# A contrast kernel on one core: the first slot of its ring holds two half tiles instead of one tile

## The chip, the cores and the metric

The kernel runs on one core of a Trainium2 chip. The other cores do nothing. The time is in device microseconds (us), lower is better; each version is run several times, and the median is taken. One further execution is recorded by the hardware profiler: its trace holds every instruction and every DMA packet with start and length.

The engines that matter here are VectorE (DVE in the profile), ScalarE (ACT), TensorE (PE), GpSimd (POOL) and SyncE (SP). SP issues the loads, ACT issues the stores, and 16 DMA engines move the bytes of both queues.

## What is computed

```python
def setup_inputs():
    batch, c, h, w = 16, 3, 512, 512
    return {
        "x": np.random.rand(batch, c, h, w).astype(np.float32),
        "factor": np.float32(1.5),
    }

def reference(x, factor):
    mean = np.mean(x, axis=(2, 3), keepdims=True)
    return np.clip(mean + factor * (x - mean), 0, 1).astype(np.float32)
```

There are 48 images (16 x 3) of 262,144 pixels in float32, 50.33 MB in and as much out. Every pixel becomes factor * x + (1 - factor) * mean of its image, held between 0 and 1. An image's mean must be known before any of its pixels can be written.

## The kernel before

The input lies in DRAM as one run of numbers. A tile is four images, 4.19 MB, spread over 128 partitions with 8192 numbers (32 KB) in each, so that one image covers 32 partitions. There are 12 tiles. A ring in SBUF, `ring` (L66), has six slots of one tile; tile t lives in slot t mod 6 and is changed in place.

The body is under `tc.manual_schedule()` (L103): the instructions of every engine stand in the order in which the program writes them, and the framework adds the semaphore waits.

- **Loads** (L68 to L76) go out on SP's queue. Tile 0 comes in two DMAs, columns 0 to 2047 (1 MB) and 2048 to 8191 (3 MB), L104 and L105; tile 1 in one; tiles 2 and 3 in one DMA of 8 MB, and tiles 4 and 5 in another (L107, L108). After computing tile t, SP is given the load of tile t + 6 (L112), which waits until the stores of tile t have read their slot. SP's queue runs in order, so a load that waits holds up the loads behind it.
- **Compute** (L78 to L98) of a tile: VectorE sums columns 0 to 4351 of each partition (L81, `SUM` = 4352) while ScalarE sums the other 3840 by an activation with an accumulator (L84; what it writes goes to `junk` and is not used). Two matrix products with the constant `blockw` (L86, L87) add the partial sums over the 32 partitions of each image, scale them by (1 - factor) / pixels, and leave the shift of each partition in PSUM (`bias`). VectorE then does x * factor + shift over the whole tile (L91) and the clamp (L94).
- **Stores** (L101) go out on ACT's queue, one DMA of 4 MB a tile. Tile 0 is the exception: `FIRST` = (2048, 6144) makes it do L91, L94 and the store for the first 2048 columns and then for the other 6144, so that it has two stores of 1 MB and 3 MB. ACT's queue holds sum, store, sum, store; the store of a tile waits for L94 of that tile.
- **Constants**: GpSimd fills `blockw` (L61, L63) at the start: zero, and four 32x32 blocks on the diagonal.

In DRAM a partition's 32 KB follow on those of the partition before. A store or load of a whole tile is therefore one unbroken stretch of 4 MB; the two parts of tile 0 take 8 KB and 24 KB out of every 32 KB.

Of the kernel before, what the change touches and what calls it, by code (L numbers as in the profile page):

```python
# [1 line left out]

# [4 lines left out]


P = 128  # L10
ROW = 8192
BUFS = 6
SHORT = 2048
FIRST = (SHORT, ROW - SHORT)
SUM = 4352


@with_exitstack
def kernel(
    ctx: ExitStack,  # L20
    tc: tile.TileContext,
    x: bass.AP,
    factor: float,
    out: bass.AP,
):

    nc = tc.nc
    f32 = mybir.dt.float32  # L30
    Alu = mybir.AluOpType
    Act = mybir.ActivationFunctionType

    B, C, H, W = x.shape
    n_img, n_pix = B * C, H * W
    ppi = n_pix // ROW
    per_tile = P // ppi
    n_tiles = n_img // per_tile
    assert ppi * ROW == n_pix and per_tile * n_tiles == n_img

    factor = float(factor)
    wconst = (1.0 - factor) / float(n_pix)

    x_f = x.rearrange("b c h w -> (b c h w)")
    out_f = out.rearrange("b c h w -> (b c h w)")

    def dram(ap, t, c0=0, c1=ROW):
        return bass.AP(tensor=ap.tensor, offset=t * P * ROW + c0, ap=[[ROW, P], [1, c1 - c0]])

    consts = ctx.enter_context(tc.tile_pool(name="consts", bufs=1))  # L50
    xpool = ctx.enter_context(tc.tile_pool(name="xpool", bufs=1))
    small = ctx.enter_context(tc.tile_pool(name="small", bufs=1))
    psum = ctx.enter_context(tc.tile_pool(name="psum", bufs=1, space=bass.MemoryType.PSUM))


    sums = small.tile([P, 2 * n_tiles], f32, name="sums")
    junk = small.tile([P, ROW - SUM], f32, name="junk")
    bias = psum.tile([P, n_tiles], f32, name="bias")

    blockw = consts.tile([P, P], f32, name="blockw")  # L60
    nc.gpsimd.memset(blockw, 0.0)  # L61
    for a in range(0, P, ppi):
        nc.gpsimd.memset(blockw[a : a + ppi, a : a + ppi], wconst)  # L63


    ring = xpool.tile([P, BUFS, ROW], f32, name="ring")  # L66

    def load(t, c0=0, c1=ROW, n=1):  # L68

        b = t % BUFS  # L70
        src = bass.AP(
            tensor=x_f.tensor,
            offset=t * P * ROW + c0,
            ap=[[ROW, P], [P * ROW, n], [1, c1 - c0]],
        )
        nc.sync.dma_start(out=ring[:, b : b + n, c0:c1], in_=src)  # L76

    def compute(t):  # L78
        xt = ring[:, t % BUFS, :]
        own = sums[:, 2 * t : 2 * t + 2]  # L80
        nc.vector.tensor_reduce(  # L81
            out=own[:, 0:1], in_=xt[:, 0:SUM], axis=mybir.AxisListType.X, op=Alu.add
        )
        nc.scalar.activation(out=junk, in_=xt[:, SUM:ROW], func=Act.Copy, accum_out=own[:, 1:2])  # L84
        shift = bias[:, t : t + 1]
        nc.tensor.matmul(shift, blockw, own[:, 1:2], start=True, stop=False)  # L86
        nc.tensor.matmul(shift, blockw, own[:, 0:1], start=False, stop=True)  # L87
        c = 0
        for n in FIRST if t == 0 else [ROW]:
            part = xt[:, c : c + n]  # L90
            nc.vector.tensor_scalar(  # L91
                out=part, in0=part, scalar1=factor, scalar2=shift, op0=Alu.mult, op1=Alu.add
            )
            nc.vector.tensor_scalar(  # L94
                out=part, in0=part, scalar1=0.0, scalar2=1.0, op0=Alu.max, op1=Alu.min
            )
            store(t, c, c + n)
            c += n  # L98

    def store(t, c0, c1):  # L100
        nc.scalar.dma_start(out=dram(out_f, t, c0, c1), in_=ring[:, t % BUFS, c0:c1])  # L101

    with tc.manual_schedule():  # L103
        load(0, c1=SHORT)  # L104
        load(0, c0=SHORT)  # L105
        load(1)
        load(2, n=2)  # L107
        load(4, n=2)  # L108
        for t in range(n_tiles):
            compute(t)  # L110
            if t + BUFS < n_tiles:
                load(t + BUFS)  # L112


# [1 line left out]
_INS = ['x', 'factor']  # L116
_OUTS = [((16, 3, 512, 512), 'float32')]

_NUMBERS = {'factor': 1.5}


# [26 lines left out]
```

## Time and profile before

| what | value |
|---|---|
| time, three runs | 239.05, 239.31, 240.11 us (median 239.31) |
| span of the profiled execution | 237.3 us |
| bytes read, written | 50.33 MB, 50.33 MB |
| mean rate over the span | 424 GB/s |
| VectorE busy | 163.1 us (69%) |
| ScalarE busy | 43.2 us (18%) |
| TensorE busy | 14.1 us (6%) |
| loads on SP, stores on ACT | 11 DMAs, 13 DMAs |

The span runs from the first to the last event of the program in the profiler's record; the time of a run is taken around it and is longer. The profiled execution is one of its own, and its time beyond the span is not recorded: 2.0 us lie between its span and the median of the three runs.

The profile's page divides the span into 40 equal slices and prints for each the busy share of each engine in tenths (9 is 90% or more) and the rate in GB/s. It lists the DMA queues with their packets; one packet is one row of a transfer, or one of 4 bytes that signals a semaphore. Then comes the chain of waits that ended last, and the groups of instructions by line, with the mean time of one. Of DMA issues it gives the time from issue to landing:

```profile
out_dram<-ring ACTq DMA_DIRECT2D x11, 4096.0 KB, 35.8
ring<-in_x_dram SPq DMA_DIRECT2D x7, 4096.0 KB, 49.7
ring<-in_x_dram SPq DMA_DIRECT2D x2, 8192.0 KB, 66.7
ring<-in_x_dram SPq DMA_DIRECT2D x1, 3072.0 KB, 11.7
out_dram<-ring ACTq DMA_DIRECT2D x1, 3072.0 KB, 28.2
ring<-in_x_dram SPq DMA_DIRECT2D x1, 1024.0 KB, 4.8
out_dram<-ring ACTq DMA_DIRECT2D x1, 1024.0 KB, 17.5
```

The columns are what is moved, the queue, how many DMAs, the size of each, and the median time to landing in us. A transfer that stands behind others in its queue shows their time too.

### The profile page before, as it was taken

The numbers are of one execution on the slowest core, as the hardware profiler recorded it, in microseconds if no ns is written. First come the engines' busy times: TensorE is split into PE (matmuls) and PEld (weight loads), VectorE is DVE, ScalarE is ACT, GpSimd is POOL, SyncE is SP. The second block draws the span as 40 slices with busy tenths as digits, with TensorE's granted clock in tenths as the row PEclk, the third lists the DMA queues.
The fourth block names the chain that finished last, engine by engine and source line by source line (L and its number), as shares of the span: only waits on it lengthen the run. The fifth ranks groups of instructions, "written<-read, shape, count | busy, mean of one in ns | idle before, by whom it ended". The sixth has DMA issues, their size and how long they took to land.

```text
span 237.3 us, 285 instructions
## 1 busy us (share of the span) xinstructions
PE 14.1 (6%) x48; PEld 12.0 (5%) x48; DVE 163.1 (69%) x38; ACT 43.2 (18%) x25; POOL 0.9 (0%) x9
## 2 busy tenths in 40 slices
PE   0010010001010001010010100100100100010000
PEld 0010010001010001010010100100100100010000
DVE  0079989048989328999989898891892795687000
ACT  2050230041050023050320504101400500500000
POOL 1000000000000000000000000000000000000000
DMA  7999999999999999999999999999999999999996
GB/s 297 410 442 442 421 442 359 456 439 441 442 436 414 403 431 442 442 442 442 436 442 436 414 409 425 442 442 442 442 436 442 436 420 403 425 442 442 442 442 265
DMA packets 3712, 100.66 MB, mean 424 GB/s; under 512 B 384, under 2 KB 384, under 8 KB 384
## 3 DMA queue, kind: packets, MB, share of 16 engines
q1 hardware_dynamic: 1840, 50.33, 49.7%
q10 hardware_dynamic: 1872, 50.33, 49.2%
HBM read 50.33 MB, written 50.33 MB: 424 GB/s over the span
## 4 chain that ended last, share of the span: by engine, by line
DMA 57%; DVE 29%; another core or an unknown queue 3%; PE 1%; SPq 1%; issue 0%; DVEq 0%
DMA ring<-in_x_dram 41%; DMA out_dram<-ring 16%; DVE sums L81 10%; DVE ring L91 9%; DVE ring L94 9%; PE bias L87 1%; SPq L76 1%; DVEq L91 0%
## 5 line engine op out<-in xcount | busy, mean ns | idle before, releaser
L81 DVE TENSOR_REDUCE sums<-ring 128x1 f32<-128x4352 f32 x12 | 56.2, 4683 | 45.7 <-DMA ring<-in_x_dram 45.7
L84 ACT ACTIVATE junk<-ring 128x3840 f32<-128x3840 f32 x12 | 40.8, 3403 | 163.3 <-DMA ring<-in_x_dram 107.5
L91 DVE TENSOR_SCALAR ring<-ring,bias 128x8192 f32<-128x8192 f32 (+2 forms) x13 | 54.1, 4163 | 8.9 <-PE bias L87 7.4
L94 DVE TENSOR_SCALAR ring<-ring 128x8192 f32<-128x8192 f32 (+2 forms) x13 | 53.3, 4099 | 0.4
L86 PE MATMUL bias<-sums,blockw 128*128 128x1 f32 x24 | 7.0, 361 | 190.8 <-ACT junk L84 190.8
L86 PEld LDWEIGHTS bias<-sums,blockw 128*128 128x128 f32 x24 | 6.0, 312 | 191.7 <-ACT junk L84 175.2
L87 PE MATMUL bias<-sums,blockw 128*128 128x1 f32 x24 | 7.0, 363 | 4.3 <-DVE sums L81 3.9
L87 PEld LDWEIGHTS bias<-sums,blockw 128*128 128x128 f32 x24 | 6.0, 311 | 5.3 <-DVE sums L81 5.0
L84 ACT ACTIVATION_READ_ACCUMULATOR junk<-ring 128x1 f32 x12 | 2.2, 186 | 0.0
L84 ACT ACT_TABLE_LOAD x1 | 1.3, 1283 | 0.7 <-PEq L129 0.7
L63 POOL MEMSET blockw<- 32x32 f32 x4 | 0.5, 117 | 0.2
L61 POOL MEMSET blockw<- 128x128 f32 x1 | 0.2, 204 | 0.3 <-POOLq L129 0.3
L129 POOL MEMSET const-bfloat16-1.0<- 128x1 bf16 x1 | 0.1, 111 | 0.0
L129 POOL MEMSET const-uint8-127<- 128x1 uint8 x1 | 0.1, 111 | 0.0
L129 POOL MEMSET const-float32-1.0<- 128x1 f32 x1 | 0.1, 108 | 0.0
L129 POOL MEMSET const-float32-0.0<- 128x1 f32 x1 | 0.1, 103 | 0.2 <-issue 0.2
## 6 DMA issues: line engine op xcount, KB each, us to landing
out_dram<-ring ACTq DMA_DIRECT2D x11, 4096.0 KB, 35.8
ring<-in_x_dram SPq DMA_DIRECT2D x7, 4096.0 KB, 49.7
ring<-in_x_dram SPq DMA_DIRECT2D x2, 8192.0 KB, 66.7
ring<-in_x_dram SPq DMA_DIRECT2D x1, 3072.0 KB, 11.7
out_dram<-ring ACTq DMA_DIRECT2D x1, 3072.0 KB, 28.2
ring<-in_x_dram SPq DMA_DIRECT2D x1, 1024.0 KB, 4.8
out_dram<-ring ACTq DMA_DIRECT2D x1, 1024.0 KB, 17.5
```

Of the source, the lines that this page charges most:

```text
L61: nc.gpsimd.memset(blockw, 0.0)
L63: nc.gpsimd.memset(blockw[a : a + ppi, a : a + ppi], wconst)
L76: nc.sync.dma_start(out=ring[:, b : b + n, c0:c1], in_=src)
L81: nc.vector.tensor_reduce(out=own[:, 0:1], in_=xt[:, 0:SUM], axis=mybir.AxisListType.X, op=Alu.add)
L84: nc.scalar.activation(out=junk, in_=xt[:, SUM:ROW], func=Act.Copy, accum_out=own[:, 1:2])
L86: nc.tensor.matmul(shift, blockw, own[:, 1:2], start=True, stop=False)
L87: nc.tensor.matmul(shift, blockw, own[:, 0:1], start=False, stop=True)
L91: nc.vector.tensor_scalar(out=part, in0=part, scalar1=factor, scalar2=shift, op0=Alu.mult, op1=Alu.add)
L94: nc.vector.tensor_scalar(out=part, in0=part, scalar1=0.0, scalar2=1.0, op0=Alu.max, op1=Alu.min)
L129: nc = _bacc.Bacc("TRN2", target_bir_lowering=False, num_devices=1)
```

## The change

The work is divided by images instead of by fixed rows. `TILES` gives the images of each tile: two tiles of two images, then eleven of four, 13 tiles in all. `IMG` = 2048 is what one image takes in every partition when it is spread over all 128, so a tile of n images has rows of n * 2048 numbers: 16 KB for the first two, 32 KB for the others. The ring becomes one run of columns; the first two tiles share slot 0, and tile 7 is the next to use that slot.

- Tiles 0 and 1 are each loaded by one DMA of 2 MB and stored by one of 2 MB. In a two-image tile an image covers 64 partitions, so there is a second constant matrix, with two 64x64 blocks.
- The loads up front are tile 0, tile 1, tile 2, tiles 3 and 4 together, tiles 5 and 6 together. Nothing is loaded after computing tile 0; after tile 1 comes the load of tile 7, which waits for the stores of both half tiles, and so on to tile 12.
- VectorE's share of the summing is 35/64 of a row: 4480 columns of 8192, and 2240 of 4096. ScalarE has the other 3712 or 1856.
- L91 and L94 (now L97 and L100) run over the whole tile in every case; the split of tile 0 is gone.

```diff
-ROW = 8192
-BUFS = 6
-SHORT = 2048
-FIRST = (SHORT, ROW - SHORT)
-SUM = 4352
+IMG = 2048
+SLOTS = 6
+
+TILES = (2, 2) + (4,) * 11
+
+SHARE = 35
...
+    first = [sum(TILES[:t]) for t in range(n_tiles)]
+    columns = SLOTS * 4 * IMG
...
+    block = {}
+    for n in sorted(set(TILES)):
+        rows = P // n
+        block[n] = m = consts.tile([P, P], f32, name=f"block{n}")
+        nc.gpsimd.memset(m, 0.0 if n > 1 else wconst)
+        for a in range(0, P, rows) if n > 1 else ():
+            nc.gpsimd.memset(m[a : a + rows, a : a + rows], wconst)
...
+    def cols(t):
+        a = first[t] * IMG % columns
+        return ring[:, a : a + TILES[t] * IMG]
...
+    def dram(ap, t, n=1):
+        row = TILES[t] * IMG
+        return bass.AP(
+            tensor=ap.tensor, offset=first[t] * n_pix, ap=[[row, P], [P * row, n], [1, row]]
+        )
...
+    def load(t, n=1):
+        a = first[t] * IMG % columns
+        row = TILES[t] * IMG
+        dst = ring[:, a : a + n * row].rearrange("p (n r) -> p n r", r=row)
+        nc.sync.dma_start(out=dst, in_=dram(x_f, t, n))
...
     def compute(t):
-        xt = ring[:, t % BUFS, :]
+        xt = cols(t)
+        row = TILES[t] * IMG
+        vec = row * SHARE // 64
...
-        c = 0
-        for n in FIRST if t == 0 else [ROW]:
-            part = xt[:, c : c + n]
-            nc.vector.tensor_scalar(
-                out=part, in0=part, scalar1=factor, scalar2=shift, op0=Alu.mult, op1=Alu.add
-            )
-            nc.vector.tensor_scalar(
-                out=part, in0=part, scalar1=0.0, scalar2=1.0, op0=Alu.max, op1=Alu.min
-            )
-            store(t, c, c + n)
-            c += n
...
+        nc.scalar.dma_start(
+            out=dram(out_f, t), in_=xt.rearrange("p (n r) -> p n r", n=1)
+        )
...
     with tc.manual_schedule():
-        load(0, c1=SHORT)
-        load(0, c0=SHORT)
+        load(0)
         load(1)
-        load(2, n=2)
-        load(4, n=2)
+        load(2)
+        load(3, n=2)
+        load(5, n=2)
         for t in range(n_tiles):
             compute(t)
-            if t + BUFS < n_tiles:
-                load(t + BUFS)
+            if t >= 1 and t + SLOTS < n_tiles:
+                load(t + SLOTS)
```

More of the change, by code (lines that the diff above doesn't have):

```diff
@@ L34 @@
     B, C, H, W = x.shape
[L35 to L39, printed above, removed]
+    n_pix = H * W
+    assert n_pix == P * IMG and sum(TILES) == B * C
     factor = float(factor)
@@ L45 @@
     out_f = out.rearrange("b c h w -> (b c h w)")
-    def dram(ap, t, c0=0, c1=ROW):
-        return bass.AP(tensor=ap.tensor, offset=t * P * ROW + c0, ap=[[ROW, P], [1, c1 - c0]])
+    n_tiles = len(TILES)
+    first = [sum(TILES[:t]) for t in range(n_tiles)]
+    columns = SLOTS * 4 * IMG
     consts = ctx.enter_context(tc.tile_pool(name="consts", bufs=1))
@@ L56 @@
     sums = small.tile([P, 2 * n_tiles], f32, name="sums")
-    junk = small.tile([P, ROW - SUM], f32, name="junk")
+    junk = small.tile([P, 4 * IMG * (64 - SHARE) // 64], f32, name="junk")
     bias = psum.tile([P, n_tiles], f32, name="bias")
[L60 to L74, printed above, removed]
-        )
-        nc.sync.dma_start(out=ring[:, b : b + n, c0:c1], in_=src)
+    block = {}
@@ new lines @@
+    for n in sorted(set(TILES)):
[4 more added lines that the diff above has]
+            nc.gpsimd.memset(m[a : a + rows, a : a + rows], wconst)
+    ring = xpool.tile([P, columns], f32, name="ring")
+    def cols(t):
[5 more added lines that the diff above has]
+            tensor=ap.tensor, offset=first[t] * n_pix, ap=[[row, P], [P * row, n], [1, row]]
+        )
@@ L78, in compute @@
+    def load(t, n=1):
[3 more added lines that the diff above has]
+        nc.sync.dma_start(out=dst, in_=dram(x_f, t, n))
     def compute(t):
-        xt = ring[:, t % BUFS, :]
+        xt = cols(t)
+        row = TILES[t] * IMG
+        vec = row * SHARE // 64
         own = sums[:, 2 * t : 2 * t + 2]
         nc.vector.tensor_reduce(
-            out=own[:, 0:1], in_=xt[:, 0:SUM], axis=mybir.AxisListType.X, op=Alu.add
+            out=own[:, 0:1], in_=xt[:, 0:vec], axis=mybir.AxisListType.X, op=Alu.add
@@ L83, in compute @@
         )
-        nc.scalar.activation(out=junk, in_=xt[:, SUM:ROW], func=Act.Copy, accum_out=own[:, 1:2])
+        nc.scalar.activation(
+            out=junk[:, 0 : row - vec], in_=xt[:, vec:row], func=Act.Copy, accum_out=own[:, 1:2]
+        )
         shift = bias[:, t : t + 1]
-        nc.tensor.matmul(shift, blockw, own[:, 1:2], start=True, stop=False)
-        nc.tensor.matmul(shift, blockw, own[:, 0:1], start=False, stop=True)
-        c = 0
-        for n in FIRST if t == 0 else [ROW]:
-            part = xt[:, c : c + n]
-            nc.vector.tensor_scalar(
-                out=part, in0=part, scalar1=factor, scalar2=shift, op0=Alu.mult, op1=Alu.add
-            )
-            nc.vector.tensor_scalar(
-                out=part, in0=part, scalar1=0.0, scalar2=1.0, op0=Alu.max, op1=Alu.min
-            )
-            store(t, c, c + n)
-            c += n
@@ L100, in store @@
-    def store(t, c0, c1):
-        nc.scalar.dma_start(out=dram(out_f, t, c0, c1), in_=ring[:, t % BUFS, c0:c1])
+        nc.tensor.matmul(shift, block[TILES[t]], own[:, 1:2], start=True, stop=False)
+        nc.tensor.matmul(shift, block[TILES[t]], own[:, 0:1], start=False, stop=True)
+        nc.vector.tensor_scalar(
+            out=xt, in0=xt, scalar1=factor, scalar2=shift, op0=Alu.mult, op1=Alu.add
+        )
+        nc.vector.tensor_scalar(
+            out=xt, in0=xt, scalar1=0.0, scalar2=1.0, op0=Alu.max, op1=Alu.min
+        )
@@ L103 @@
+        nc.scalar.dma_start(
+            out=dram(out_f, t), in_=xt.rearrange("p (n r) -> p n r", n=1)
+        )
     with tc.manual_schedule():
-        load(0, c1=SHORT)
-        load(0, c0=SHORT)
+        load(0)
         load(1)
-        load(2, n=2)
-        load(4, n=2)
+        load(2)
+        load(3, n=2)
+        load(5, n=2)
         for t in range(n_tiles):
             compute(t)
-            if t + BUFS < n_tiles:
-                load(t + BUFS)
+            if t >= 1 and t + SLOTS < n_tiles:
+                load(t + SLOTS)
```

## The prediction, made before the change was run

> **What bounds the kernel now.** I read the time slices first, then the DMA part, then busy time in three long stretches, and only then the chain of waits.
>
> ```profile
> DVE  0079989048989328999989898891892795687000
> ...
> DMA  7999999999999999999999999999999999999996
> ...
> DMA packets 3712, 100.66 MB, mean 424 GB/s; under 512 B 384, under 2 KB 384, under 8 KB 384
> ...
> DMA 57%; DVE 29%; another core or an unknown queue 3%; PE 1%; SPq 1%; issue 0%; DVEq 0%
> ```
>
> The DMA engines are busy in every slice but the two at the ends; VectorE has holes of whole slices. So the chain's "DVE 29%" misleads: a chain must pass through some work, but while VectorE computes, the 16 engines move other tiles. What counts is bytes over rate plus the moments when the engines are not full.
>
> ```profile
> 0.00:60.00 60.00, 3.49 (x12) 3.01 (x12) 35.98 (x10) 11.77 (x7) 0.88 (x9) 1.00 0.97 411
> 60.00:203.70 143.70, 9.39 (x32) 8.02 (x32) 113.49 (x26) 27.97 (x16) 0.00 (x0) 1.00 1.01 434
> 203.70:237.30 33.60, 1.18 (x4) 1.01 (x4) 13.60 (x3) 3.50 (x2) 0.00 (x0) 1.00 0.94 406
> ```
>
> The columns are stretch, length, busy time of the engines, clock, DMA share and GB/s. With both streams running the rate is 434. At that rate 100.66 MB take 100.66/0.434 = 231.9 us; the span is 237.3, so 5.4 us are lost in all: 60 x (1 - 411/434) = 3.2 in the first 60 us, 33.6 x (1 - 406/434) = 2.2 in the last stretch, none between. The packet records of the same trace (start, length, bytes, queue) place them. At the start: first packet at 1.74 us, then 0.7 until all engines run at their usual packet time. Near 24 to 28 us and 37.7 to 39.3 us, 0.8 together: load packets of 32 KB, otherwise 1.213 us, take up to 1.508 and 1.792. At the end: 0.4 because the engines do not finish together and 1.25 after the last packet (236.05). These are 4.9 of the 5.4; the rest is rounding and edges of the windows.
>
> ```profile
> 12.96 4.69 DVE L81 TENSOR_REDUCE sums<-ring 128x1 f32<-128x4352 f32 x1 [12.96 <-DMA ring<-in_x_dram]
> 20.91 7.06 ACTq L101 DMA_DIRECT2D out_dram<-ring  x2
> 41.94 0.34 ACTq L101 DMA_DIRECT2D out_dram<-ring  x1
> 203.76 4.69 DVE L81 TENSOR_REDUCE sums<-ring 128x1 f32<-128x4352 f32 x1 [4.98 <-DMA ring<-in_x_dram]
> 218.17 0.34 ACTq L101 DMA_DIRECT2D out_dram<-ring  x1
> ```
>
> Tile 0 is there at 12.96, its stores are issued at 20.9 and 27.6 (20.91 + 7.06 - 0.34), tile 1's at 41.94. The last load lands at 203.7, the last store is issued at 218.2.
>
> **The change part by part.**
>
> *Transfers.* Before: 11 loads and 13 stores. After: 5 loads up front and 6 later, 13 stores. The number of DMAs stays 24, and the bytes stay. Rows: 128 of 8 KB and 128 of 24 KB become 256 of 16 KB, each way; 3712 packets stay 3712. Packet times of the records: 8 KB 0.309, 24 KB 0.912, 32 KB 1.213 us; 16 KB, the mean of the first two, 0.610. Each engine has 8 rows of each: 8 x (0.309 + 0.912) = 9.77 against 16 x 0.610 = 9.76. Cost 0.0.
>
> *Compute.* Reduce: 4683 ns x 4480/4352 = 4.82 for a full tile, x 2240/4352 = 2.41 for a half one. 4096 columns lie midway between the 2048 and 6144 rows: (1291 + 3418)/2 = 2.36 for L91's operation, (1227 + 3359)/2 = 2.29 for L94's. VectorE: 2 x (2.41 + 2.36 + 2.29) + 11 x (4.82 + 4.49 + 4.43) = 165.3 against 163.1, so 2.2 more. ScalarE's 128x3840 at 3.40 becomes 3.29 and twice 1.64. One tile more costs PE two further products (0.6 each) and VectorE a 0.7 wait for them. All this lies beside transfers, since the DMA engines hold 434 GB/s whether VectorE works or not; uncovered it would be about 3 us. GpSimd's three added memsets (0.1 to 0.2 each, rows of L61 and L63) end near 2 us, long before the first product.
>
> *Order at the start.* Half of tile 0's 4.19 MB lands 2.1/0.434 = 4.8 us earlier, at 8.1. VectorE: 8.1 + 2.41 + 0.7 + 2.36 + 2.29 = 15.9, the first store's issue (was 20.9). Tile 1 (landed by 12.9) then ends at 23.7, its store is issued there (was 27.6). Tile 2 (landed near 22.6) takes 4.82 + 0.75 + 4.49 + 4.43 and its store goes at 38.2 (was 41.94).
>
> *Stores beside loads.* The first store's first packet came 3.7 us after issue (24.64), and its eight rows per engine took until 36.9: 12.3 us, which is 8 x (0.309 + 1.213), one store row and one load row in turn. With 16 KB rows: 8 x (0.610 + 1.213) = 14.6. So store 0 runs 19.6 to 34.2, store 1, after the 1.4 us that lay between the two stores before, 35.6 to 50.2, and it lands 1.5 later (36.9 to 38.4 before): 51.7. The whole slot was free at 55.9 before.
>
> The Trainium skill, "DMA: Bandwidth & Descriptors", section "Queues, rings and completion order", says that an engine serves its queue rows in turn, a packet of typically 9 to 17 descriptors at a time. By that a half tile's 8 rows would drain in one turn, 8 x 0.610 = 4.9 us, and the slot would be free some 20 us sooner; the row just read shows one row a turn. The sum would be the same by either, since the engines are full.
>
> *The wait moved on SP.* Tile 7's load waits for both half stores. Queued behind it on SP are loads 8 to 12, which wait for later stores anyway, and compute 7 waits for it. Issued at 51.7 (tile 6's was at 55.9), it stands behind tiles 5 and 6, 8.4 MB not yet moved; nobody feels it. ACT's queue holds the same sequence, sum then store.
>
> *The moments that are not full.* This is all that can move. The start (0.7) does not depend on row size as far as rows show; it may vanish or grow by as much. The slow spells at 24 to 28 and 37.7 to 39.3, 0.4 each, stood where the two short-row stores of tile 0 began, and at no later store. What they are the trace does not tell. They may go (-0.8: after the change each store is one unbroken stretch of DRAM, and no store of a whole tile shows a spell) or come three times at their largest packet excess, 1.792 - 1.213 = 0.58 (two short-row stores and store 3, which may find its queue empty near 70): 3 x 0.58 - 0.8 = +0.9. The nearest rows are two short-row stores with one spell each, and there are again two: I take 0. The tail: the same last 4 MB in 32 KB rows, 0.
>
> *The end.* Earlier stores take bytes from loads. By 50.7 the stores have moved 4.2 MB instead of 1.05 + 3.15 x (50.7 - 38.3)/16 = 3.5, so loads are up to 0.7 MB behind, 3.2 us at their half of the rate: the last lands by 207.0, and the last store is issued 14.6 later, at 221.6. The store ahead of it keeps the engines busy to 236.05 - 8 x 1.213 = 226.3. Cover 4.7 us (8.1 before): nothing lost.
>
> Sum: 237.3 + 0.0 (rows) + 0.0 (compute) + 0.0 (order) + 0.0 (spells) = 237.3. The median of the runs stands 2.0 above that span, so **239.3 us**.
>
> **The rivals.** *The start gets cleaner.* The spells go (-0.8) and the slow first packets, 8 KB rows of a strided region until now, too (up to -0.7): 237.3 - 1.5 + 2.0 = 237.8. For it: every spell stands beside rows shorter than 32 KB. Against it: the first packets need not be slow for their rows, and 16 KB rows are short as well.
>
> *The end runs dry.* If loads fall behind by 2.2 MB (a whole half tile) rather than 0.7, the last lands 10 us late, at 213.7; its store is issued at 228.3, after the engines have emptied at 226.3; with 1.0 to the first packet (0.74 to 1.74 at the start), 9.7 of packets and 1.25 after, the span is 240.2, the time 242.2. It decides once the last landing passes 211.8. Against it: both streams get equal turns from 52 us on, and slot releases come earlier, not later.
>
> *The earlier store shortens the run* by the 5.0 us of its head start: 234.3. Against it: the engines were full between 15.9 and 20.9 too, so a store there only displaces a load.
>
> **How the numbers follow.** Measurements of this kernel tell apart about 0.5%, 1.2 us. Forecast (238.1 to 240.5): 0.73. Cleaner start, or more by the third rival: 0.15. End dry, or spells at every store beyond their bound: 0.12. The range 238.0 to 240.4 takes in -0.8 and +0.9 for the spells with part of the start's 0.7, and leaves under 2 in 10 outside.
>
> **What would show it.** Right: 434 GB/s from 60 us to the last landing, first store at 16, the slot's reload near 52, last landing 204 to 207. Wrong: a DMA slice under 9 inside the run, a last store issued after 226, or spells much longer or gone.

## The result, and the profile after

| | before | changed |
|---|---|---|
| median of 12 runs | 239.24 us | 242.58 us |
| lowest to highest | 239.04 to 240.11 | 239.45 to 243.31 |
| span of the profiled execution | 237.3 us | 240.9 us |

The ratio is 1.0114, 95% interval 1.009 to 1.0138: slower by about one per cent, where no change had been forecast. The second row matters as much: the kernel before repeats within half a per cent, the changed one does not, and two of its 12 runs are where the forecast put it (239.45, 239.82), with a third between (240.89). Ratios leave out executions more than 1.5% above a kernel's fastest; since scatter is part of what was found here, the medians and ranges below are over all executions, which all ran at the same clock (1.00).

From the page of the changed kernel, the time slices, the DMA line and the chain of waits:

```profile
DVE  0498886008898908998989986894787489189200
...
DMA  7999999999999999999999999999999999999993
...
DMA packets 3712, 100.66 MB, mean 418 GB/s; under 512 B 384, under 2 KB 384, under 8 KB 384
...
DVE 32%; another core or an unknown queue 7%; PE 1%; issue 1%; DVEq 0%
```

The DMA issues, with sizes and the median time from issue to landing:

```profile
out_dram<-ring ACTq DMA_DIRECT2D x11, 4096.0 KB, 30.5
ring<-in_x_dram SPq DMA_DIRECT2D x7, 4096.0 KB, 57.8
ring<-in_x_dram SPq DMA_DIRECT2D x2, 8192.0 KB, 70.4
ring<-in_x_dram SPq DMA_DIRECT2D x2, 2048.0 KB, 10.0
out_dram<-ring ACTq DMA_DIRECT2D x2, 2048.0 KB, 22.7
```

The median store lands 5.3 us sooner after its issue than before (30.5 against 35.8), the median load 8.1 us later (57.8 against 49.7): less stands ahead of a store in its queue, and more ahead of a load. Packets and bytes are as before, and the DMA engines are again busy in every slice; only the last slice fell from 6 to 3. The chain names VectorE and no DMA at all: it is of no use here. The three stretches, cut at the last load's landing as before:

```profile
0.00:60.00 60.00, 3.89 (x14) 3.44 (x14) 32.69 (x10) 11.74 (x9) 1.25 (x12) 1.00 0.98 411
60.00:209.80 149.80, 9.97 (x34) 8.52 (x34) 118.50 (x27) 27.12 (x16) 0.00 (x0) 1.00 1.00 429
209.80:240.90 31.10, 1.17 (x4) 1.00 (x4) 13.74 (x3) 3.39 (x2) 0.00 (x0) 1.00 0.87 377
```

Measured against 434 GB/s, the stretches lose 3.2, 149.8 x (1 - 429/434) = 1.7 and 31.1 x (1 - 377/434) = 4.1 us; before it was 3.2, 0.0 and 2.2. So the 3.6 us come half from the steady middle, where nothing had been lost, and half from the end.

The packet records say what this is. Two sums are made of them: the time by which packets exceed their usual length, and the time in which fewer than 16 packets are under way, each divided by 16.

```
lost, us                                     before  changed  difference
start: slow packets and engines not yet busy   0.69     1.19      +0.50
slow packets where the first stores begin      0.81     0.57      -0.24
slow packets later (changed: 108 to 193 us)    0.01     1.52      +1.51
engines idle at the end, others still moving   0.38     2.19      +1.81
sum                                            1.89     5.47      +3.58
```

The same is seen in the semaphore records. Each of the 16 engines signals its own share of a DMA. For the last store of the changed kernel these signals come from 236.7 to 240.0 us; before, from 235.8 to 236.4. The engines had drifted apart. During the run the time from the first to the last signal of one load (below: how far the engines are apart) grows period by period.

```
changed: load landed at    90.4  109.8  130.1  150.6  170.4  190.2  209.8
         first to last      0.78   0.83   1.59   2.61   2.93   3.21   3.29
before:  load landed at    87.6  106.9  126.3  145.6  165.0  184.4  203.7
         first to last      1.77   1.79   1.77   1.77   1.76   1.79   1.77
```

The Trainium skill, "DMA: Bandwidth & Descriptors", section "Why a DMA increments its semaphore by 16 and not by 1", states that the engines of one DMA finish independently and are counted by the semaphore; these records agree, with up to 3.3 us between them.

The slow packets of the changed kernel stand, with few exceptions, in clusters: at 108 to 117, 128 to 137, 147 to 156, 167 to 175 and 187 to 193. Each lies where a load DMA passes to the next one (call it a changeover), followed closely by a changeover of the stores. By packet starts, new load rows begin at 110.0, 129.4 and 148.9, new store rows at 112.4, 131.8 and 151.4: 2.4 us apart, one row of each queue (1.213 each). In the kernel before, 106.0 and 115.0 lie 9.0 apart. This time, from the first new load row to the first new store row, is called the distance below. Theory A of the experiments is that a short distance makes packets slow and sets the engines apart; theory B, that the 16 KB rows do.

Why the distance changed: the half tiles' stores start and end sooner, and store 3 comes late, onto an empty store queue.

```profile
8.55 2.49 DVE L88 TENSOR_REDUCE sums<-ring 128x1 f32<-128x2240 f32 x1 [8.55 <-DMA ring<-in_x_dram]
...
16.52 0.38 ACTq L103 DMA_DIRECT2D out_dram<-ring  x1
24.74 0.34 ACTq L103 DMA_DIRECT2D out_dram<-ring  x1
...
40.11 0.34 ACTq L103 DMA_DIRECT2D out_dram<-ring  x1
55.23 4.82 DVE L88 TENSOR_REDUCE sums<-ring 128x1 f32<-128x4480 f32 x1 [15.15 <-DMA ring<-in_x_dram]
...
69.79 0.34 ACTq L103 DMA_DIRECT2D out_dram<-ring  x1
...
209.80 4.82 DVE L88 TENSOR_REDUCE sums<-ring 128x1 f32<-128x4480 f32 x1 [5.08 <-DMA ring<-in_x_dram]
...
224.36 0.34 ACTq L103 DMA_DIRECT2D out_dram<-ring  x1
```

These are timeline lines (start, length, what): the first half tile at 8.55, the stores of tiles 0 to 3, the last load and the last store. The first engine ends its share of store 2 at 69.1 and the last one at 70.3; store 3 is issued at 69.79 and its first packet starts at 73.5. From there on both queues take turns, and the distance set here stays for the rest of the run. It is a knob: delaying that store by some time moves its changeovers later and, since loads run alone meanwhile, theirs earlier, so the distance moves by about twice the delay.

### The profile page after: what moved, and what is told of

Same layout as the page of the kernel before. It is cut to its first block, busy times and chain, and to the rows that moved or that the text cites. A ratio compares the mean times of both kernels' runs of the same rounds, so it can differ in the third digit from the quotient of the medians.

```text
span 240.9 us, 303 instructions
## 1 busy us (share of the span) xinstructions
PE 15.0 (6%) x52; PEld 13.0 (5%) x52; DVE 164.9 (68%) x39; ACT 42.3 (18%) x27; POOL 1.3 (1%) x12
## 2 busy tenths in 40 slices
DMA packets 3712, 100.66 MB, mean 418 GB/s; under 512 B 384, under 2 KB 384, under 8 KB 384
## 5 line engine op out<-in xcount | busy, mean ns | idle before, releaser
L88 DVE TENSOR_REDUCE sums<-ring 128x1 f32<-128x4480 f32 (+1 forms) x13 | 57.9, 4457 | 48.8 <-DMA ring<-in_x_dram 48.8
L91 ACT ACTIVATE junk<-ring 128x3712 f32<-128x3712 f32 (+1 forms) x13 | 39.8, 3059 | 170.3 <-DMA ring<-in_x_dram 118.6
L97 DVE TENSOR_SCALAR ring<-ring,bias 128x8192 f32<-128x8192 f32 (+1 forms) x13 | 54.1, 4163 | 10.2 <-PE bias L96 9.4
L100 DVE TENSOR_SCALAR ring<-ring 128x8192 f32<-128x8192 f32 (+1 forms) x13 | 53.3, 4099 | 0.4
L95 PE MATMUL bias<-sums,block 128*128 128x1 f32 x26 | 7.6, 360 | 193.4 <-ACT junk L91 186.2
L95 PEld LDWEIGHTS bias<-sums,block 128*128 128x128 f32 x26 | 6.5, 310 | 194.4 <-ACT junk L91 174.7
L96 PE MATMUL bias<-sums,block 128*128 128x1 f32 x26 | 7.6, 362 | 6.8 <-DVE sums L88 6.8
L96 PEld LDWEIGHTS bias<-sums,block 128*128 128x128 f32 x26 | 6.6, 314 | 7.8 <-DVE sums L88 7.7
L91 ACT ACTIVATION_READ_ACCUMULATOR junk<-ring 128x1 f32 x13 | 2.4, 187 | 0.0
L63 POOL MEMSET block<- 32x32 f32 (+1 forms) x6 | 0.8, 126 | 0.2
## 6 DMA issues: line engine op xcount, KB each, us to landing
out_dram<-ring ACTq DMA_DIRECT2D x11, 4096.0 KB, 30.5
ring<-in_x_dram SPq DMA_DIRECT2D x7, 4096.0 KB, 57.8
```

Of the source, the lines that this page charges most:

```text
L63: nc.gpsimd.memset(m[a : a + rows, a : a + rows], wconst)
L88: nc.vector.tensor_reduce(out=own[:, 0:1], in_=xt[:, 0:vec], axis=mybir.AxisListType.X, op=Alu.add)
L91: nc.scalar.activation(out=junk[:, 0 : row - vec], in_=xt[:, vec:row], func=Act.Copy, accum_out=own[:, 1:2])
L95: nc.tensor.matmul(shift, block[TILES[t]], own[:, 1:2], start=True, stop=False)
L96: nc.tensor.matmul(shift, block[TILES[t]], own[:, 0:1], start=False, stop=True)
L97: nc.vector.tensor_scalar(out=xt, in0=xt, scalar1=factor, scalar2=shift, op0=Alu.mult, op1=Alu.add)
```

## The experiments

Each kernel was timed in up to 11 executions beside the kernel before on the same chip, which stayed at a median of 239.2 to 239.3 throughout; of its 78 executions none took more than 239.9. Distances, landings and engines are those of the one profiled execution of each kernel. The first four look for what matters: row length, half tiles, or the distance.

**e1: tile 0 of the kernel before in two strided halves.**

```diff
-SHORT = 2048
+SHORT = 4096
```

> Theory A (changeover): in the changed kernel a load DMA and a store DMA change over on the engines within 2.4 us of each other in every 19.6 us period (load rows of a new tile start at 90.5, 110.0, 129.4; store rows at 92.9, 112.4, 131.8), against 9.0 us in the kernel before (106.0 and 115.0), and packets are slow at those points alone. Here tile 0 of the kernel before is moved in two halves of 16 KB rows cut out of its 32 KB rows; its stores end about 3 us later than before, which moves the changeovers further apart, to about 15 us: no slow packets after 60 us, time 239.0 to 240.0. Theory B (rows of 16 KB): the short rows set the engines apart at the start and they stay apart: first to last engine over 2.5 us at the last landing, time 241.5 to 243.

Measured 239.12 (239.03 to 239.30), ratio 0.9996, interval 0.9988 to 1.0005. Distance 12.1 us, engines 0.4 us apart at every landing. Rows of 16 KB as such cost nothing.

**e2: twelve tiles of four images.**

```diff
-TILES = (2, 2) + (4,) * 11
+TILES = (4,) * 12
...
-        load(2)
-        load(3, n=2)
-        load(5, n=2)
+        load(2, n=2)
+        load(4, n=2)
...
-            if t >= 1 and t + SLOTS < n_tiles:
+            if t + SLOTS < n_tiles:
```

> The changed kernel with twelve tiles of four images and no half tile. Theory B: no short rows, so no spells and 238.5 to 239.5. Theory A: the only store of the first slot goes out near 27.6 and ends near 50.7, 3.6 us earlier than the two stores of the kernel before, which brings the changeovers from 9.0 to about 2 us apart: spells in each period after 100 us, 241.5 to 243 in most executions.

Measured 240.25 (239.43 to 240.80). Distance 1.2 us, the engines 2.1 us apart at 112 us and 2.8 at 190. These are the signals of stores; those of loads lie 1.3 us apart at 111 us and 1.0 at 188. With no half tile a part of the loss is there, less than theory A's 241.5 to 243 and more than theory B's 238.5 to 239.5, and with few slow packets (0.23 us after 60 us).

**e3: the changed kernel, store 3 three us later.**

```diff
-    sums = small.tile([P, 2 * n_tiles], f32, name="sums")
+    sums = small.tile([P, 2 * n_tiles + 1], f32, name="sums")
...
+        if t == 3:
+            nc.vector.tensor_reduce(
+                out=sums[:, 2 * n_tiles :], in_=xt[:, 0:3000], axis=mybir.AxisListType.X, op=Alu.add
+            )
         shift = bias[:, t : t + 1]
```

> The changed kernel with one extra VectorE sum of 3000 columns (about 3.2 us) in tile 3, whose store starts on an empty queue at 73.5. The store starts 3.2 us later and the loads, alone meanwhile, get 3.2 us further: changeovers 2.4 + 6.4 = about 9 us apart as in the kernel before. Theory A: no spells after 100 us, 239.0 to 240.0 although work was added. Theory B: 242 to 243 as in the changed kernel.

Measured 239.80 (239.45 to 240.40): adding work took 2.8 us away. Load rows start at 106.2, store rows at 114.8; 0.09 us of slow packets after 60 us, and engines that stay 2.2 to 2.4 us apart.

**e4: the changed kernel with single loads.**

```diff
-        load(3, n=2)
-        load(5, n=2)
+        load(3)
+        load(4)
+        load(5)
+        load(6)
```

> The changed kernel with tiles 3, 4, 5 and 6 loaded one by one. Tile 3 lands some 8 us earlier, so its store follows store 2 without the empty stretch of 69.1 to 73.5: the store starts about 3 us earlier and the changeovers lie about 6 us further the other way, near -3.5 (16 of 19.6). Theory A: few spells, 239 to 240.5. Theory B: 242 to 243.

Measured 239.85 (239.77 to 240.16). Here the store changes over first, 4.9 us ahead of the load; engines 0.8 us apart throughout.

The next four turn the knob, in the kernel before as well.

**f1: the kernel before, tile 2's store late** (three sums of 4352 columns, at t == 2, in the manner of e3's edit).

> The kernel before, nothing of the change in it, with three extra VectorE sums (14 us) in tile 2, so that its store starts on an empty queue near 82.7 instead of 76.3. The changeovers, 9.0 us apart before, move by twice the 6.4 us: 21.8, which is 2.4 after one period of 19.4. Theory A (distance of the changeovers): slow packets in each later period and engines drifting apart, 240.5 to 243. Theory C (it belongs to the changed kernel's start: its 2 MB loads and first stores set the engines apart, and the distance of the changeovers is not what matters): 239.0 to 239.6 as before.

Measured 240.18, and from 239.45 to 248.28: between the ranges of theories A and C. Without the three executions above 244 us the ratio is 1.0032 (interval 1.0016 to 1.0048). In the profiled execution, one of the three (span 242.4), the distance was 1.6 us and then 2.5, and the engines went from 1.8 us apart at 101 us to 5.9 at 183. The stretches of this execution, for comparison with those of the kernel before:

```profile
0.00:60.00 60.00, 3.49 (x12) 3.00 (x12) 36.62 (x10) 11.77 (x7) 0.89 (x9) 1.00 0.98 411
60.00:203.10 143.10, 9.38 (x32) 8.02 (x32) 126.74 (x30) 28.10 (x17) 0.00 (x0) 1.00 1.00 427
203.10:242.40 39.30, 1.18 (x4) 1.01 (x4) 13.41 (x3) 3.36 (x2) 0.00 (x0) 1.00 0.88 381
```

The first line is as before; the loss is again in the middle (427 for 434) and at the end. The trouble does not need the change, though most executions of f1 have little of it.

**f2, f3, f4: store 3 of the changed kernel later by 1.3, 7.4 and 8.6 us of extra sums** (1100 columns; twice 3400; twice 4000).

> The changed kernel with an extra sum of 1100 columns (1.3 us) in tile 3: changeovers 2.4 + 2.6 = 5.0 us apart. Theory A: few slow packets, 239.5 to 240.5; if the harm reaches over two rows, 240.5 to 242. Theory C: 242 to 243.

> The changed kernel with 7.4 us more in tile 3: changeovers 2.4 + 14.8 = 17.2 us apart, that is 2.2 the other way, the store first. Theory A in its plain form (near is bad, whichever comes first): 241 to 243. If only a load just ahead of a store is bad: 239.5 to 240.2. Theory C: 242 to 243.

> The changed kernel with 8.6 us more in tile 3: changeovers 2.4 + 17.2 = 19.6, together. Theory A: 240.5 to 243, packets slow at the common changeover. Theory C: 242 to 243.

f2: 241.04 (240.68 to 242.18), distance 4.5, engines from 1.9 us apart to 3.0 at the last landing, with only 0.08 us of slow packets after 60 us: here the engines drift without them. f3: 240.05 (239.67 to 240.25), the store first by 3.4, engines steady at 1.85. f4: 240.00 (239.88 to 240.47). It did not come to lie together: the store changed over first by 2.4, engines steady at 1.45. So in these runs a store just ahead of a load does no harm; a load just ahead of a store does.

**g1: tile 0 of the twelve-tile form loaded in two DMAs of 64 partitions.** This and the next two turn to the start and to the changed kernel itself.

```diff
+    def load_part(p0, p1):
+        row = TILES[0] * IMG
+        src = bass.AP(tensor=x_f.tensor, offset=p0 * row, ap=[[row, p1 - p0], [1, row]])
+        nc.sync.dma_start(out=ring[p0:p1, 0:row], in_=src)
...
-        load(0)
+        load_part(0, 64)
+        load_part(64, 128)
```

> The twelve-tile form with tile 0 loaded in two DMAs of 64 partitions, each one unbroken stretch of 2 MB in 32 KB rows. In the executions so far the first 4.19 MB have landed at 12.9 to 13.0 where the first DMA's rows span 4 MB (kernel before, strided halves, twelve tiles) and at 13.3 to 13.7 in the six with two stretches of 2 MB, in which neighbouring engines start 128 KB instead of 256 KB apart. If the stretch matters: 13.3 to 13.7 here too, and 0.3 to 0.6 us more than the twelve-tile form with the same later part. If the 16 KB rows matter: 12.9 to 13.1.

Measured 250.90 (250.41 to 251.24): the question was not answered, because something larger came in. (How far apart in DRAM neighbouring engines start no trace shows; the packets are recorded without addresses.) While half the partitions are written, the rate is half:

```profile
6.00:12.00 6.00, 0.00 (x0) 0.00 (x0) 0.00 (x0) 0.00 (x0) 0.00 (x0) 1.00 0.93 191
12.00:22.00 10.00, 0.00 (x0) 0.00 (x0) 0.00 (x0) 0.00 (x0) 0.00 (x0) 1.00 1.00 210
22.00:42.00 20.00, 0.98 (x4) 0.93 (x4) 17.03 (x4) 7.46 (x4) 0.00 (x0) 1.00 0.99 416
```

The DMA share stands at 0.93 to 1.00 all along (last column but one), so a busy engine need not be a fast one.

**g2: the twelve-tile form, tile 2's store later** (4300 columns at t == 2).

> The twelve-tile form, whose changeovers lie 1.2 us apart and which took 240.25, with 4.6 us more VectorE work in tile 2, so that its store starts about 4 us later and the changeovers lie 9 us apart as in the kernel before. Theory A: engines stay together and 239.0 to 239.5, with more work than the form that took 240.25. Theory C: 240 or more.

Measured 240.20 (239.47 to 240.53), a miss: the median did not fall. The profiled execution was the lowest, 239.47, with a distance of 6.0 us and engines at a steady 1.4 to 1.6. What the longer ones did isn't known.

**g3: the changed kernel again.**

> The changed kernel once more, for a second profile. Theory A: changeovers again 2 to 3 us apart, engines drift; if this execution is one of the short ones (near 239.5), either the distance differs or the engines were closer together when the changeovers began.

Eight executions from 239.29 to 252.04, median 242.78; the profiled one was the lowest.

```profile
0.00:60.00 60.00, 4.47 (x16) 3.93 (x16) 33.20 (x11) 11.75 (x9) 1.26 (x12) 1.00 0.98 411
60.00:207.70 147.70, 9.39 (x32) 8.03 (x32) 118.01 (x27) 27.12 (x16) 0.00 (x0) 1.00 1.00 433
207.70:237.50 29.80, 1.17 (x4) 1.00 (x4) 13.73 (x3) 3.39 (x2) 0.00 (x0) 1.00 0.94 405
```

The same program, span 237.5 and the middle at 433 instead of 429. Its tile 3 landed at 54.0 instead of 55.2, store 3's first packet started at 72.3 instead of 73.5, and the distance became 1.2 instead of 2.4. The engines stayed 0.66 us apart to the end. One row sooner or later at 70 us went with 3.4 us at the end.

**h1 and h2: the first two loads as every second row** (h1 on e4, h2 on the changed kernel).

```diff
+        src = dram(x_f, t, n)
+        if t < 2:
+            src = bass.AP(tensor=x_f.tensor, offset=t * row, ap=[[2 * row, P], [P * row, 1], [1, row]])
...
-        nc.sync.dma_start(out=dst, in_=dram(x_f, t, n))
+        nc.sync.dma_start(out=dst, in_=src)
```

> The form with tiles 3 to 6 loaded one by one (239.85), with the two first loads taken as every second 16 KB row of the first 4 MB, as the kernel with strided halves takes them (239.12): same bytes, same row length, another pattern in DRAM. The rows then fall into other images, so the first four images' means and places differ. If the unbroken 2 MB pattern costs the start its 0.4 us: the first 4.19 MB land at 12.9 to 13.1 instead of 13.5, and 239.3 to 239.5. If not: 13.3 to 13.7 and 239.8.

> The changed kernel with only that in its two first loads (the same images differ). Its two profiles had changeovers 2.4 us apart with the engines 1.9 us apart at the landing of 55 us (240.9 us span, drifting), and 1.2 us apart with the engines 0.65 apart (237.5, no drift). If the start sets the engines apart and the near changeovers only widen it: mostly 239.2 to 240. If the near changeovers alone make the drift: median still 241.5 to 243.

In both the first 4.19 MB landed 0.3 to 0.5 us sooner (13.0 and 13.1), so the pattern does matter there. But h1 took 239.89 (239.68 to 240.45), no less than e4: in its profile, its longest execution (240.45), the slow packets at the first stores were 0.95 us instead of e4's 0.61. And h2 took 243.34 (242.99 to 243.73): distance 2.5, engines 0.6 us apart at 90 us and 3.4 at the end. So the pattern of the first loads is not what makes the drift. With this edit the first four images' pixels are summed and placed as if they belonged to other images: h1 and h2 move the same bytes, but give other values there than the reference.

**i1 and i2: store 3 later still, by 9.8 and 11.0 us** (twice 4550 and twice 5140 columns), to bring the distance round to where it began.

> The changed kernel with 9.8 us more in tile 3. With 8.6 us more the store changed over 2.4 us ahead of the load and it took 240.0; 1.2 us more moves this by 2.4: together. The distances 1.2 and 4 to 5 (load first) took 240.25 and 241.0, 2.4 took 242.6. Theory A (distance, worst at one row of each queue, load first): 239.8 to 240.8.

> The changed kernel with 11.0 us more in tile 3: the changeovers come round to 2.4 us apart with the load first, as in the changed kernel itself, a period later. Theory A: engines drift again, 241.5 to 243.5. If delay as such heals, whatever the distance: 240.0.

i1: 241.46, from 239.94 to 250.42. In the profiled execution (span 247.3) the distance was 2.3 and the engines went from 2.2 us apart at 101 us to 10.6 at the last landing. It was one of three executions above 246 us; without these the ratio is 1.0048 (interval 1.0029 to 1.0068). The median lies above theory A's 239.8 to 240.8, but the distance of 0 which that range was worked out for was not reached. The last stretch:

```profile
207.70:247.30 39.60, 1.17 (x4) 1.00 (x4) 13.74 (x3) 3.39 (x2) 0.00 (x0) 1.00 0.76 327
```

Fifteen engines have signalled the last store by 239.8 us, the last one at 246.4: its last rows go out alone, one packet at a time, at 27 GB/s. i2: 241.92 (240.75 to 250.50); its profiled execution, the shortest, fell on 4.8 us and did not drift. By the medians 7 to 9 us of delay heal and 10 to 11 bring the trouble back: it is not the delay as such. Of these two, only the profile of i1 shows the drift itself.

All profiles together, ordered by distance (positive: the load changes over first; times in us):

```
kernel             distance   engines apart, early -> late   median (range)
h1, e4           -5.7, -4.9   2.3 -> 2.3, 0.8 -> 0.8         239.89, 239.85
f3, f4           -3.4, -2.4   1.8 -> 1.9, 1.4 -> 1.4         240.05, 240.00
g3 (changed)        1.2       0.7 -> 0.7                     this one 239.29
e2 (its stores)     1.2       2.1 -> 2.8                     240.25 (239.43 to 240.80)
g1                  1.5       1.7 -> 2.5                     250.90 (start at half rate)
i1                  2.3       2.2 -> 10.6                    241.46 (239.94 to 250.42)
changed             2.4       0.8 -> 3.3                     242.58 (239.45 to 243.31)
h2                  2.5       0.9 -> 3.4                     243.34 (242.99 to 243.73)
f1 (before)      1.6, 2.5     1.8 -> 6.5                     240.18 (239.45 to 248.28)
f2                  4.5       1.9 -> 3.0                     241.04 (240.68 to 242.18)
i2                  4.8       1.3 -> 1.3                     241.92 (240.75 to 250.50)
g2, e3            6.0, 8.6    1.6 -> 1.4, 2.2 -> 2.4         240.20, 239.80
before, e1        9.0, 12.1   1.8 -> 1.8, 0.4 -> 0.4         239.24, 239.12
```

Every profile with the load 1.5 to 4.5 us ahead drifts; none does with the store ahead or with 6 us and more. At 1.2, g3 does not and in e2 the stores do and the loads do not; at 4.8, i2 does not. No form beat the kernel before; e1 equals it.

## Why the prediction was wrong

**What held.** Rows and packet counts cost nothing in themselves (3712 packets, e1). Compute stayed hidden: VectorE at 164.9 us busy, 165.3 worked out. The order came as worked out: first store at 16.5 (15.9), second half store's packets 35.2 to 49.7 (35.6 to 50.2), the slot free at 51.3 (51.7). One row a turn is confirmed by that. The end did not run dry: the last store is issued at 224.4, 2.3 us before the first engine has finished the store ahead (226.7; the cover worked out was 4.7), and its packets follow without a gap. The earlier first store brought nothing by itself, as said of the third rival. And in the one profiled execution whose engines don't drift the changed kernel takes what was forecast: 239.29. Its 239.45 and 239.82 lie there too, without a profile.

**The step that failed** is "the moments that are not full. This is all that can move", with 0 for the spells and 0 for the tail ("the same last 4 MB"). It counted slow packets only where a store starts beside loads and put their bound at +0.9; in the changed kernel they came, +1.51, at changeovers in the middle of the run, where before there were none. And it treated 16 engines as one server. They are 16 queues with fixed shares, eight rows each of every tile; one that loses time keeps its rows while the others finish (in i1 one engine still had five rows to move when the other fifteen were done), so a drift is paid at the end: +1.81. The working had what the distance is made of on the page (store 1's end at 50.2, where the trace of before has 54.5, and store 3, which "may find its queue empty near 70"), but priced the empty store queue at one more spell, 0.58 at most. What it changes is where the two queues stand to each other afterwards. A smaller misreading: the two spells of the kernel before, "0.4 each", are 0.28 and 0.54; their sum of 0.8 is right.

**Shown:** that moving the distance moves the time, in both kernels. The kernel before, without any of the change, is made erratic by moving it (f1), the changed one is healed by it (e3, e4, f3, f4) and made ill again (i1, and by its median i2). One execution of each was profiled; the distances of the others are not known. **Not shown:** what in the engines does it at a load's end one or two rows ahead of a store's. The Trainium skill, "DMA: Bandwidth & Descriptors", section "Queues, rings and completion order", says that an engine's semaphore increment lands only after its earlier writes across its queues; two of them close together could hold an engine up. No run was made to test it, and g3 speaks against its plain form: there the signals of a load and of a store come within 0.2 us of each other in every period, and nothing drifts. **Open too:** the healed forms stay 0.6 to 0.8 us above the kernel before. Slower first packets (+0.5 in the changed kernel) are part of it, but h1 took most of these away (0.86 us lost at the start against 1.18 in e4) and gained nothing; and g2's median has no explanation.

Of the rivals, the one on the slower side had the wrong place: it waited for the last load to fall behind, and landings did come later (209.8 against 207.0 at most), but as a result of the drift: the first engine signals that load at 206.5, and in g3, without drift, it lands at 207.7.

## What to carry to other kernels

Where two DMA streams saturate the engines, "the engines are busy anyway" does not make an order free: look at the spread between the first and the last engine of each DMA, early and late, and at where load and store DMAs change over relative to each other. A small shift at a point where one queue runs empty fixes that distance for the rest of the run; if a saturated kernel scatters by more than a per cent, delay one store by a few us on purpose and see whether it settles (it did in e3, f3 and f4; g2's median did not move). The loads issued singly (e4) settled the changed kernel without extra work.

## What the runs showed of the hardware that was not expected

Loading into 64 partitions at a time ran at 191 to 210 GB/s with all engines busy: a 32 KB packet took 2.56 us (median between 12 and 22 us) instead of 1.213.

Executions of one program differ by what happens in one row: in the changed kernel's two profiles tile 3 lands 1.2 us apart, and they end 3.4 us apart. In f1, i1, i2 and g3 single executions reached 248 to 252 us, and the profile of i1 shows what such an execution consists of: a single engine still at work for 6.6 us after the other fifteen have finished.

The first 4.19 MB landed at 13.3 to 13.7 us where they came as two unbroken stretches of 2 MB, and at 12.8 to 13.1 where the first DMAs' rows spanned 4 MB.
